# A depthwise convolution issued to VectorE one instruction at a time, paced by the matmuls traced, instead of as one late block

## The chip, the core and the metric

The kernel runs on one core of a Trainium2 chip. A core has a matrix engine (TensorE, PE in the profile), a vector engine (VectorE, DVE), a scalar engine (ScalarE, ACT), GpSimd (POOL) and SyncE (SP), which here mostly issues DMAs. Each engine works through its own list of instructions in the order of the program; engines wait for each other by semaphores. The metric is the device time of one execution in microseconds (us), taken as the median of several runs.

## The reference

One decoder layer, for 1024 prompt tokens and 64 sample tokens (8 requests of 8), 1088 columns in all, in fp32:

```python
xn = rmsnorm(x, norm1_g)
q, k, v, glu_a, glu_b, gate_a, gate_b = jnp.split(xn @ w_in, SPLIT_IDX, axis=-1)
branch_a = attend(q, k, v, window=128, sinks) @ w_o_attn      # 16 query heads, 4 kv heads
u = glu_a * jax.nn.sigmoid(glu_b)                             # the gated branch, 1024 channels
c = dwconv_valid(concat([past, u]), conv_b_w, conv_b_bias)    # 31 taps, each channel by itself
branch_b = jax.nn.silu(layernorm(c, ln_b_g, ln_b_b)) @ w_pb
h = x + (sigmoid(gate_a) * branch_a + sigmoid(gate_b) * branch_b) @ w_out
y = rmsnorm(h + conv_ffn(rmsnorm(h, norm2_g)), norm_f_g)
```

The change concerns `c`, the convolution over 31 taps of the 1024 channels of `u`.

## The kernel before

Channels lie on the 128 partitions, tokens along the free dimension. Every fp32 product is three matmuls of rounded operands: high word of the weight with high word of the input, high with low, low with high (L200, L201, L202, in `mm3`). A weight block is split into its two words when it is near its turn: ACT writes the high word `whi` (L181), DVE the low word `wlo` (L182), one *unit* ahead of the unit that multiplies by it.

The input projection is a list of units, in the order of a table: 8 blocks of `glu_b` and `glu_a` (b, a), q, k, v, and 16 gates (g). A unit is one block of 128 output columns: `stream` runs over three pieces of 384, 384 and 320 tokens and, in each, over 8 blocks of the contraction. A piece has one of four PSUM buffers called `mm`, which is read out by ACT or DVE and then used again four pieces later. Four more, called `aux`, serve the attention. The two v units stand in a loop of their own, `do_v`: 9 products of 128 tokens by 256 columns, each split into two words by ACT and DVE (`split_ps`, L229 and L230). The gate units and q units of this stage are called by their letters below; "the q stage" is the run of q and k units of the second half of the heads, from about 347 us to 440 us.

The attention steps (scores, softmax, transposes of the probabilities `p`, their split into `pth` and `ptl` at L229 and L230, and the product with v that gives `av`, L385) hang on an agenda: `tick`, called by `stream` once for every three matmuls, issues those that are due between the matmuls of the units.

When a block of `glu_a` is done, `a_done` calls `conv(i, u)` for its 128 channels. It writes, all on DVE: two products and two sums for the sample tokens (L486, L487), one sum of odd and even columns (L488), 44 multiply-adds over 512 columns (L480, tiles `bt`, `c`), four closing instructions (L499 to L502); ACT writes three start values, and POOL's queue stores the result for the LayerNorm, which loads it at about 633 us. So 53 DVE instructions a block, 424 over the 8 blocks.

The text of the program is not the order of the engines' lists: a scheduler at build time places each instruction by a number, its priority, which grows as the program is traced, and by its own estimate of when engines are free. `later(off)` adds an offset to that number:

```python
with self.later(CONV_LATER):      # CONV_LATER = 1200
    self.conv(i, u)
```

So before the change the whole convolution of a block is traced at once and stands 1200 numbers later: the scheduler puts its instructions where it believes DVE is free.

Of the kernel before, what the change touches and what calls it, by code (L numbers as in the profile page):

```python
# [70 lines left out]
MEAN_LATER = (100, 100, 100)  # L71
W_PARTS = 4
PIECES = {384: 3, 320: 4, 432: 4, 256: 2, 272: 4}
CONV_LATER = 1200
LN_STEPS = (0, 7, 15)
LN_LEAD = -4
LN_SPACING = 15
# [4 lines left out]
def weight_order():  # L82
    order, count = [], {}
    gates = [(kind, i) for i in range(KT) for kind in ("ga", "gb")]
    for w in SEQUENCE:
        n = count[w] = count.get(w, -1) + 1
        if w == "g":
            order.append(gates.pop(0))
        elif w[0] == "q":
            order.append(("q", (int(w[1]), n)))  # L90
        elif w[0] == "k":
            order.append(("k", int(w[1])))
        else:
            order.append((w, n))
    assert not gates
    n_in = len(order)
    order += [("o", m) for m in range(KT)]
    order += [("pb", m) for m in PB_ORDER]
    order += [("out", m) for m in range(KT)]
    for f in range(NF):  # L100
        order += [("up", f), ("up", NF + f)]
    order += [("dn", f) for f in range(NF)]
    return order, n_in
# [16 lines left out]
class Build:  # L120
    def __init__(self, tc, a):
        self.tc, self.nc, self.a = tc, tc.nc, a
        self.order, self.n_in = weight_order()
        self.uid = 0
        self.agenda, self.now = [], 0

    @contextmanager
    def later(self, off):
# [329 lines left out]
    def tick(self, upto=None):  # L458
        self.now = self.now + 1 if upto is None else upto
        while self.agenda and self.agenda[0][0] <= self.now:  # L460
            self.agenda.pop(0)[1]()

    def drain(self):
        while self.agenda:
            self.agenda.pop(0)[1]()


    def conv(self, i, u):
        nc = self.nc
        half = SEQ // 2  # L470
        acc = self.t(self.cv, [P, T], "c")
        sm = self.t(self.cv, [P, half + 15], "sm")
        bt = self.t(self.cv, [P, half + 1], "bt")
        us = u[:, PW:].rearrange("p (b t) -> p b t", b=NB)
        sp = acc[:, SEQ:].rearrange("p (b t) -> p b t", b=NB)
        ev, od = u[:, 0:PW:2], u[:, 1:PW:2]
        ye, yo = acc[:, 0:SEQ:2], acc[:, 1:SEQ:2]
        h = lambda k: self.c("cw", i * CW + k)
        hs = lambda j: self.hsum[:, 16 * i + j:16 * i + j + 1]
        mac = lambda o, x, w: nc.vector.scalar_tensor_tensor(o, x, w, o, ALU.mult, ALU.add)  # L480
        taps = self.c("cw", i * CW, CW)[:, None, None, :].to_broadcast([P, NB // 2, NT, CW])
        prod = acc[:, 0:NS // 2 * CW].rearrange("p (b t k) -> p b t k", b=NB // 2, k=CW)
        for x in range(2):
            win = us[:, 4 * x:4 * x + 4, 0:NT]
            win = bass.AP(tensor=win.tensor, offset=win.offset, ap=[list(z) for z in win.ap] + [[1, CW]])
            nc.vector.tensor_tensor(prod, win, taps, ALU.mult)  # L486
            nc.vector.tensor_reduce(sp[:, 4 * x:4 * x + 4, :], prod, AX.X, ALU.add)  # L487
        nc.vector.tensor_tensor(sm, od[:, 0:half + 15], ev[:, 1:half + 16], ALU.add)  # L488
        act = nc.scalar.activation
        act(bt, ev[:, 0:half + 1], AF.Identity, scale=h(0))  # L490
        act(ye, od[:, 0:half], AF.Identity, bias=self.c("cb", i), scale=h(1))
        act(yo, sm[:, 0:half], AF.Identity, bias=self.cb2[:, i:i + 1], scale=hs(0))
        for j in range(1, 16):
            mac(bt, ev[:, j:j + half + 1], h(2 * j))
            if j < 15:
                mac(ye, od[:, j:j + half], h(2 * j + 1))
            mac(yo, sm[:, j:j + half], hs(j))
        out = u[:, NS:NS + SEQ]
        nc.vector.tensor_scalar(u[:, 0:NS], acc[:, SEQ:], self.c("cb", i), None, ALU.add)  # L499
        nc.vector.tensor_tensor(yo, yo, bt[:, 1:], ALU.subtract)  # L500
        nc.vector.tensor_tensor(out[:, 1::2], yo, ye, ALU.subtract)
        nc.vector.tensor_tensor(out[:, 0::2], ye, bt[:, 0:half], ALU.add)  # L502
        nc.gpsimd.dma_start(self.d_c[i, :, 0:SEQ], out)
        nc.gpsimd.dma_start(self.d_c[i, :, SEQ:], u[:, 0:NS])
# [116 lines left out]
    def folds(self, n_dn):  # L621
        wall = self.a["wall"]

        def stages(n):
            x, y = wall[n_dn + 2 * n], wall[n_dn + 2 * n + 1]
            return self.fold_stages(x[:, :HW], y[:, :HW], x[:, HW:], y[:, HW:], self.d_wd[n])

        ticks = [[] for _ in range(NF - PLAIN)]
        for n in range(NP):
            for k, stage in enumerate(stages(n)):  # L630
                ticks[n * (NF - PLAIN - 6) // (NP - 1) + k] += stage
        for tick in ticks:
            self.fold(tick)
            yield

    def pool(self, es, name, side="right", bufs=1):
        return es.enter_context(self.tc.tile_pool(name=name, bufs=bufs, side=side, reuse_waits="tile"))

    def phase_x(self):
# [14 lines left out]
        def u_views(u):  # L654
            return u[:, PW:].rearrange("p (b t) -> p b t", b=NB)

        def u_start(i):
            u = self.t(self.cv, [P, UW], "u", bufs=2)
            nc.gpsimd.memset(u[:, 0:HIST], 0.0)
            nc.gpsimd.memset(u[:, HIST + SEQ:PW], 0.0)  # L660
            nc.sync.dma_start(u_views(u)[:, :, 0:HIST], a["cbT"][i])
            return u
# [23 lines left out]
        def a_done(i, u):  # L686
            us = u_views(u)
            nc.gpsimd.dma_start(a["o_cbp"][i], u[:, SEQ:SEQ + HIST])
            nc.gpsimd.dma_start(a["o_cbs"][i], us[:, :, NT:])
            with self.later(CONV_LATER):  # L690
                self.conv(i, u)

        def do_b(i):
            u = u_start(i)
            self.stream(("b", i), xs, b_evac(u))
            gate_u(u)
            return u

        def do_a(i, u):
            self.stream(("a", i), xs, a_evac(u))  # L700
            a_done(i, u)
# [108 lines left out]
        while len(self.w_raw) < FIRST:  # L810
            self.w_load()
        xr.append(self.norm1_load(p0, 2))
        u = u_start(0)
        a_t = self.t(self.cv, [P, T], "c")
        self.scale = None
# [34 lines left out]
        for d, x, y, r in u_part(u, 0, T):  # L850
            nc.vector.tensor_tensor(d, d, r(a_t[:, x:y]), ALU.mult)
        a_done(0, u)
        self.scale = None
        p0_es.close()
# [9 lines left out]
        for n, (kind, i) in enumerate(self.order[:self.n_in]):  # L864
# [16 lines left out]
            if kind == "b":  # L881
                u = do_b(i)
# [19 lines left out]
    def phase_y(self, right, a0_es, states, ah, al):  # L902
        nc, tc, a, pool = self.nc, self.tc, self.a, self.pool
        s_es = ExitStack()
        sp = pool(s_es, "s", "left")
        sh, sl = self.act_tiles(sp, "s")
        bh, bl = states[1]["q"]

        def xa(c, k):
            o, n = CHUNKS[c]  # L910
            h, l = (ah, al) if k < 4 else (bh, bl)
            return h[:, k % 4, o:o + n], l[:, k % 4, o:o + n]

        def do_o(m):
            t = self.t(self.lt, [P, T], "ga", bufs=2)
            nc.sync.dma_start(t, self.d_ga[m])
            nc.scalar.activation(t, t, AF.Sigmoid)

            def ev(c, o, n, ps):
                r = self.t(self.lt, [P, 384], "ma", bufs=2)  # L920
                nc.vector.tensor_tensor(r[:, :n], ps[:, :n], t[:, o:o + n], ALU.mult)
                nc.gpsimd.dma_start(self.d_ma[m, :, o:o + n], r[:, :n])

            self.stream(("o", m), xa, ev)

        steps = []
        for x in range(KT):
            steps += self.ln_steps(x, self.now + LN_LEAD + x * LN_SPACING, sh, sl)
        self.plan(steps)
        for m in range(KT):  # L930
            do_o(m)
        self.drain()
        a0_es.close()
        right.close()
        self.phase_z(s_es, sh, sl)
# [855 lines left out]
```

## Time and profile before

| | |
|---|---|
| time, median of 3 runs (lowest, highest) | 1659.28 us (1658.15, 1660.51) |
| the profiled execution | 1659.53 us, span 1657.8 us, granted clock 0.997 |
| PE busy | 1642.9 us, 99% of the span |
| DVE busy | 1336.1 us, 81% |
| ACT busy | 893.3 us, 54% |
| POOL busy | 328.1 us, 20% |
| input projection with attention and convolution | about 45 to 616 us |

The times of the trace start with the span, which is 1.7 us shorter than the execution that it belongs to. A row of the timeline gives an instruction's start, its length, its engine, its line, and in brackets the idle time ahead of it and what ended that. A matmul's length covers more than its turn: the turns are read from the starts (384 columns: 0.173 us apart). The same holds on DVE, where a multiply-add is 0.75 us long, and the next starts 0.67 us after it.

### The profile page before, as it was taken

What the parts mean: (1) busy time and instruction counts of PE and PEld (TensorE: products, weight loads), DVE (VectorE), ACT (ScalarE), POOL (GpSimd) and SP (SyncE); (2) the same over time, 40 slices, a digit from 0 to 9 for tenths busy, and PEclk for the clock granted to TensorE, in tenths of its full rate; (3) what the DMA queues carried; (4) which work ended last, traced back from release to release, by engine and by line L of the source; (5) the groups of instructions that cost most, each with busy time, mean ns of one, the idle gap of its engine ahead of it and who ended that gap; (6) DMA issues with size and microseconds to landing.
All of it is one profiled execution on the core that took longest, in us unless ns stands there. A gap on an engine that the chain in (4) does not pass through costs nothing.

```text
span 1657.8 us, 30344 instructions
## 1 busy us (share of the span) xinstructions
PE 1642.9 (99%) x11616; PEld 1627.3 (98%) x11616; DVE 1336.1 (81%) x2430; ACT 893.3 (54%) x1817; POOL 328.1 (20%) x589
## 2 busy tenths in 40 slices
PE   9999999999999999999999999999999999999998
PEld 9999999999999999999999999999999999999997
DVE  8899999999769995866685897877777777977556
ACT  7434477753488754993343564444444446834322
POOL 1210114171211211110000123333433220000050
PEclk9999999999999999999999999999999999999999
DMA  6122216254421255545346527676777544857473
GB/s 213 43 52 71 60 63 167 62 178 103 115 67 47 83 195 184 165 137 190 113 136 194 134 79 204 183 182 176 182 176 176 144 112 149 286 157 218 138 148 117
DMA packets 121313, 232.12 MB, mean 140 GB/s; under 512 B 25408, under 2 KB 67536, under 8 KB 120736
## 3 DMA queue, kind: packets, MB, share of 16 engines
q1 hardware_dynamic: 88208, 140.14, 27.6%
q0 software_dynamic: 32384, 89.51, 21.3%
q8 instruction: 91, 1.49, 0.4%
q10 hardware_dynamic: 576, 0.53, 0.1%
q14 instruction: 54, 0.44, 0.1%
HBM read 169.74 MB, written 89.62 MB: 156 GB/s over the span
## 4 chain that ended last, share of the span: by engine, by line
PE 81%; DVE 11%; ACT 4%; issue 2%; DMA 1%; POOL 0%; SPq 0%; DVEq 0%; ACTq 0%; POOLq 0%
PE mm L200 19%; PE mm L202 19%; PE mm L201 19%; PE aux L200 6%; PE aux L202 6%; PE aux L201 6%; DVE c L480 3%; DVE bt L480 2%; PE aux L366 1%; ACT p L332 1%; ACT p L336 1%; PE aux L378 1%; DVE wlo L182 1%; PE aux L356 1%; PE aux L379 1%
## 5 line engine op out<-in xcount | busy, mean ns | idle before, releaser
L200 PE MATMUL mm<-xh,whi 128*128 128x384 f32 (+1 forms) x920 | 306.6, 333 | 0.6 <-ACT whi L181 0.6
L201 PE MATMUL mm<-xl,whi 128*128 128x384 f32 (+1 forms) x920 | 301.1, 327 | 0.0
L202 PE MATMUL mm<-xh,wlo 128*128 128x384 f32 (+1 forms) x920 | 300.7, 327 | 0.0
L200 PEld LDWEIGHTS mm<-xh,whi 128*128 128x128 f32 x920 | 173.3, 188 | 2.2 <-ACT whi L181 1.2
L201 PEld LDWEIGHTS mm<-xl,whi 128*128 128x128 f32 x920 | 173.4, 188 | 1.0
L202 PEld LDWEIGHTS mm<-xh,wlo 128*128 128x128 f32 x920 | 173.1, 188 | 0.1
L1209 DVE SCALAR_TENSOR_TENSOR acc<-st,fc,acc 128x1104 f32<-128x1104 f32 x88 | 119.5, 1361 | 8.7 <-ACT acc L1207 7.9
L181 ACT CAST whi<-wraw 128x1024 fp32r<-128x1024 f32 (+1 forms) x65 | 62.7, 970 | 56.8 <-PE mm L201 44.6
L480 DVE SCALAR_TENSOR_TENSOR bt<-u,consts,bt 128x513 f32<-128x513 f32 x120 | 89.7, 747 | 0.6
L480 DVE SCALAR_TENSOR_TENSOR c<-sm,hsum,c 128x512 f32<-128x512 f32 x120 | 89.4, 745 | 0.5
L182 DVE TENSOR_TENSOR wlo<-wraw,whi 128x1024 fp32r<-128x1024 f32 (+1 forms) x65 | 72.5, 1121 | 20.1 <-ACT whi L181 19.6
L480 DVE SCALAR_TENSOR_TENSOR c<-u,consts,c 128x512 f32<-128x512 f32 x112 | 83.5, 745 | 0.2
L229 ACT CAST wlo<-th 128x512 fp32r<-128x512 f32 x56 | 35.1, 626 | 65.0 <-PE aux L202 41.3
L1378 ACT COPY st<-mm 128x272 f32<-128x272 f32 (+2 forms) x133 | 44.4, 350 | 46.8 <-PE mm L202 46.8
L200 PE MATMUL mm<-th,whi 128*128 128x272 f32 x240 | 69.3, 289 | 0.0
L202 PE MATMUL mm<-th,whi 128*128 128x272 f32 x240 | 69.3, 289 | 0.0
L201 PE MATMUL mm<-tl,whi 128*128 128x272 f32 x240 | 69.1, 288 | 0.0
L332 ACT ACTIVATE p<-p,nm 128x257 f32<-128x257 f32 (+1 forms) x128 | 62.2, 490 | 11.0 <-DVE nm L327 10.1
L1357 DVE TENSOR_TENSOR st<-st,aux 128x272 f32<-128x272 f32 (+2 forms) x95 | 34.2, 378 | 38.5 <-PE aux L202 38.5
L202 PE MATMUL mm<-sh,wlo 128*128 128x384 f32 (+1 forms) x192 | 62.6, 326 | 0.0
L201 PE MATMUL mm<-sl,whi 128*128 128x384 f32 (+1 forms) x192 | 62.6, 326 | 0.0
L200 PE MATMUL mm<-sh,whi 128*128 128x384 f32 (+1 forms) x192 | 62.6, 326 | 0.0
(651 smaller groups left out, 5906.8 us busy)
## 6 DMA issues: line engine op xcount, KB each, us to landing
wraw<-wall SPq DMA_DIRECT2D x87, 512.0 KB, 4.0
d_x<-st POOLq DMA_DIRECT2D x27, 544.0 KB, 4.9
d_wd<-wall POOLq DMA_DIRECT2D x54, 256.0 KB, 6.1
th<-wall SPq DMA_DIRECT2D x18, 512.0 KB, 6.0
wraw<-wall SPq DMA_DIRECT2D x33, 256.0 KB, 4.1
x<-d_x SPq DMA_DIRECT2D x14, 544.0 KB, 4.8
d_x<-acc POOLq DMA_DIRECT2D x9, 816.0 KB, 7.2
d_wo<-wall POOLq DMA_DIRECT2D x24, 256.0 KB, 4.9
```

Of the source, the lines that this page charges most:

```text
L181: self.nc.scalar.copy(h[:, z], r[:, z])
L182: self.nc.vector.tensor_tensor(l[:, z], r[:, z], h[:, z].bitcast(F32), ALU.subtract)
L200: mm(ps, wh, xh, start=first, stop=False, skip_group_check=more)
L201: mm(ps, wh, xl, start=False, stop=False, skip_group_check=more)
L202: mm(ps, wl, xh, start=False, stop=last, skip_group_check=more)
L229: self.nc.scalar.copy(h, src)
L332: nc.scalar.activation(pt[:, j, lo:width + 1], pt[:, j, lo:width + 1], AF.Exp, bias=nm[:, j:j + 1], scale=-1.0, accum_out=den[:, j:j + 1])
L336: nc.scalar.activation(pt[:, j, lo:width], pt[:, j, lo:width], AF.Identity, scale=den[:, j:j + 1])
L480: mac = lambda o, x, w: nc.vector.scalar_tensor_tensor(o, x, w, o, ALU.mult, ALU.add)
L1209: self.last_tap = nc.vector.scalar_tensor_tensor(acc, st[:, k:k + AW], fw(f, k), acc, ALU.mult, ALU.add)
L1357: plus = lambda d, s: nc.vector.tensor_tensor(d, d, s, ALU.add)
L1378: op(d, r(ps))
```

## The change

`conv` becomes a generator, which stops after each of its DVE instructions (some stops hold two). `a_done` only puts it on a list. `tick`, after the attention steps that are due, calls a new function `pace`. This looks at the instructions traced since the last call: each of PE adds 0.172 to an account, each of DVE takes 0.5 off; the account is capped at 1.4, and while it is above zero, one step of the oldest convolution is issued and 0.68 taken off. Each step is tied (`issue_after`) behind the DVE instruction traced last, with an offset of 30 instead of 1200. Starting a new block of `glu_b` first issues what is left of all convolutions but the last, and the phase after the projection issues everything that is left.

```diff
-CONV_LATER = 1200
+PE_STEP, DVE_STEP, CONV_STEP = 0.172, 0.5, 0.68
+ROOM = 1.4
+PACE_LATER = 30
...
     def tick(self, upto=None):
...
             self.agenda.pop(0)[1]()
+        self.pace()
+
+    def pace(self):
+
+        traced, pe, dve = self.nc.cur_bb.bb.instructions, self.nc.tensor.engine, self.nc.vector.engine
+        for ins in list(traced)[self.seen:]:
+            if ins.engine == pe:
+                self.room += PE_STEP
+            elif ins.engine == dve:
+                self.room -= DVE_STEP
+        self.seen = len(traced)
+        self.room = min(self.room, ROOM) if self.convs else 0
+        while self.convs and self.room > 0:
+            self.conv_step()
+            self.room -= CONV_STEP
+        self.seen = len(traced)
+
+    def conv_step(self):
+        with ExitStack() as es:
+            dve = self.nc.vector.engine
+            es.enter_context(self.tc.issue_after(next(x for x in reversed(list(self.nc.cur_bb.bb.instructions)) if x.engine == dve)))
+            es.enter_context(self.later(PACE_LATER))
+            if next(self.convs[0], None) is None:
+                self.convs.pop(0)
+
+    def conv_flush(self, keep=0):
+        while len(self.convs) > keep:
+            self.conv_step()
...
         for j in range(1, 16):
+            yield 1
             mac(bt, ev[:, j:j + half + 1], h(2 * j))
+            yield 1
             if j < 15:
                 mac(ye, od[:, j:j + half], h(2 * j + 1))
+                yield 1
             mac(yo, sm[:, j:j + half], hs(j))
...
         def u_start(i):
+            self.conv_flush(1)
...
-            with self.later(CONV_LATER):
-                self.conv(i, u)
+            self.convs.append(self.conv(i, u))
```

Every engine gets the same instructions as before; only their order differs. The first place is DVE's list around the v products, which before stand between multiply-adds of the convolution (L480; `wlo` is the low word of a weight, L327 a row of scores). `do_v` does not call `tick`. Before:

```order
L230 TENSOR_TENSOR v_944<-mm_1856,v_944 128x2x128
L480 SCALAR_TENSOR_TENSOR bt_1131<-u_947,consts_77,bt_1131 128x513
L480 SCALAR_TENSOR_TENSOR c_1129<-u_947,consts_77,c_1129 128x512
L480 SCALAR_TENSOR_TENSOR c_1129<-sm_1130,hsum_86,c_1129 128x512
L480 SCALAR_TENSOR_TENSOR bt_1131<-u_947,consts_77,bt_1131 128x513
L230 TENSOR_TENSOR v_944<-mm_1883,v_944 128x2x128
L480 SCALAR_TENSOR_TENSOR c_1129<-sm_1130,hsum_86,c_1129 128x512
L499 TENSOR_SCALAR u_947<-c_1129,consts_77 128x64
L500 TENSOR_TENSOR c_1129<-c_1129,bt_1131 128x512
L502 TENSOR_TENSOR u_947<-c_1129,bt_1131 128x512
L230 TENSOR_TENSOR v_944<-mm_1910,v_944 128x2x128
```

The same place now (the lines are numbered anew: L480 is L512, L230 is L233, L182 is L185, L327 is L330):

```order
L512 SCALAR_TENSOR_TENSOR c_1457<-u_886,consts_77,c_1457 128x512
L233 TENSOR_TENSOR v_883<-mm_1663,v_883 128x2x128
L233 TENSOR_TENSOR v_883<-mm_1690,v_883 128x2x128
L233 TENSOR_TENSOR v_883<-mm_1717,v_883 128x2x128
L233 TENSOR_TENSOR v_883<-mm_1744,v_883 128x2x128
L233 TENSOR_TENSOR v_883<-mm_1771,v_883 128x2x128
L233 TENSOR_TENSOR v_883<-mm_1798,v_883 128x2x128
L233 TENSOR_TENSOR v_883<-mm_1825,v_883 128x2x128
L233 TENSOR_TENSOR v_883<-mm_1852,v_883 128x2x128
L185 TENSOR_TENSOR wlo_185_1917<-wraw_1657,whi_184_1916 128x1024
```

All eight v splits stand in a row, with no step of the convolution between them. What was between them stands later in DVE's list.

The second place is DVE's list in the q stage, around the 25th low word of the projection, before (L728 splits a piece of q):

```order
L480 SCALAR_TENSOR_TENSOR bt_4194<-u_4012,consts_77,bt_4194 128x513
L480 SCALAR_TENSOR_TENSOR c_4192<-u_4012,consts_77,c_4192 128x512
L728 TENSOR_TENSOR q_518_4254<-mm_4418,q_518_4254 64x256
L182 TENSOR_TENSOR wlo_535_4453<-wraw_4354,whi_534_4452 128x1024
L728 TENSOR_TENSOR q_519_4255<-mm_4418,q_519_4255 64x256
L480 SCALAR_TENSOR_TENSOR c_4192<-sm_4193,hsum_86,c_4192 128x512
```

and now (L728 is L768):

```order
L512 SCALAR_TENSOR_TENSOR c_4210<-u_3979,consts_77,c_4210 128x512
L768 TENSOR_TENSOR q_515_4193<-mm_4385,q_515_4193 64x256
L185 TENSOR_TENSOR wlo_535_4425<-wraw_4313,whi_534_4424 128x1024
L768 TENSOR_TENSOR q_516_4194<-mm_4385,q_516_4194 64x256
L512 SCALAR_TENSOR_TENSOR c_4210<-sm_4211,hsum_86,c_4210 128x512
```

Here the two lists look alike again. How many of the 424 instructions of the convolution stand ahead of a given instruction in DVE's list:

| instruction | starts before the change at | ahead, before | ahead, now |
|---|---|---|---|
| the last v split | 187.49 us | 108 | 84 |
| 15th low word | 278.89 us | 174 | 146 |
| 19th low word | 345.49 us | 218 | 202 |
| 20th low word | 359.86 us | 234 | 229 |
| 25th low word | 422.54 us | 299 | 300 |
| 34th low word | 561.54 us | 361 | 370 |

So the multiply-adds taken out of the v products are all put in again by the 25th low word, most of them between the 15th and the 20th.

More of the change, by code (lines that the diff above doesn't have):

```diff
@@ L125, in __init__ @@
         self.agenda, self.now = [], 0
+        self.convs, self.seen, self.room = [], 0, 0
     @contextmanager
@@ L493, in conv @@
         for j in range(1, 16):
+            yield 1
             mac(bt, ev[:, j:j + half + 1], h(2 * j))
+            yield 1
             if j < 15:
                 mac(ye, od[:, j:j + half], h(2 * j + 1))
+                yield 1
             mac(yo, sm[:, j:j + half], hs(j))
+        yield 1
         out = u[:, NS:NS + SEQ]
@@ L500, in conv @@
         nc.vector.tensor_tensor(yo, yo, bt[:, 1:], ALU.subtract)
+        yield 1
         nc.vector.tensor_tensor(out[:, 1::2], yo, ye, ALU.subtract)
+        yield 1
         nc.vector.tensor_tensor(out[:, 0::2], ye, bt[:, 0:half], ALU.add)
@@ L924, in do_o @@
             self.stream(("o", m), xa, ev)
+        self.conv_flush()
         steps = []
```

## The prediction

> **What bounds the kernel now.** I read the page's engine table and the chain first, then busy time by stage, then the places where PE waits.
>
> ```profile
> PE 1642.9 (99%) x11616; PEld 1627.3 (98%) x11616; DVE 1336.1 (81%) x2430; ACT 893.3 (54%) x1817; POOL 328.1 (20%) x589
> ...
> PE 81%; DVE 11%; ACT 4%; issue 2%; DMA 1%; POOL 0%; SPq 0%; DVEq 0%; ACTq 0%; POOLq 0%
> PE mm L200 19%; PE mm L202 19%; PE mm L201 19%; PE aux L200 6%; PE aux L202 6%; PE aux L201 6%; DVE c L480 3%; DVE bt L480 2%; PE aux L366 1%; ACT p L332 1%; ACT p L336 1%; PE aux L378 1%; DVE wlo L182 1%; PE aux L356 1%; PE aux L379 1%
> ```
>
> PE is idle for 1657.8 − 1642.9 = 14.9 us of the span, so no order of instructions can gain much; it can lose more. DVE is on the chain with 11%, and the multiply-adds of the convolution (L480) are its largest rows there. Where, the stretches of the input projection tell (PE, PEld, DVE, ACT, POOL busy, clock, DMA share, GB/s):
>
> ```profile
> core 0: us, PE busy (x) PEld busy (x) DVE busy (x) ACT busy (x) POOL busy (x), PEclk, DMA share, GB/s
> ...
> 150.00:190.00 40.00, 40.00 (x310) 40.00 (x310) 39.97 (x65) 8.95 (x19) 3.92 (x8) 1.00 0.23 61
> 190.00:250.00 60.00, 57.61 (x360) 55.58 (x359) 59.24 (x141) 46.22 (x123) 11.08 (x18) 0.97 0.20 62
> 250.00:300.00 50.00, 49.94 (x325) 48.36 (x325) 47.83 (x107) 41.21 (x105) 17.78 (x33) 1.00 0.55 139
> 300.00:347.00 47.00, 47.00 (x306) 45.39 (x305) 44.87 (x103) 34.55 (x87) 13.38 (x27) 1.00 0.40 107
> 347.00:385.00 38.00, 38.00 (x235) 37.96 (x234) 37.84 (x59) 12.36 (x21) 26.59 (x30) 1.00 0.53 160
> 385.00:442.00 57.00, 57.00 (x349) 57.00 (x348) 53.47 (x79) 19.02 (x38) 8.99 (x16) 1.00 0.42 101
> 442.00:485.00 43.00, 42.83 (x276) 41.87 (x274) 19.67 (x60) 34.69 (x93) 6.36 (x13) 1.00 0.38 95
> 485.00:545.00 60.00, 59.90 (x392) 57.93 (x391) 58.06 (x135) 51.04 (x129) 9.85 (x18) 1.00 0.17 47
> 545.00:605.00 60.00, 59.92 (x387) 58.04 (x386) 57.91 (x129) 46.16 (x119) 10.74 (x21) 1.00 0.31 99
> ```
>
> From 150 to 442 us both engines are nearly full: in 292 us PE lacks 2.4 us and DVE 0.03 + 0.76 + 2.17 + 2.13 + 0.16 + 3.53 = 8.8 us. Only in 442 to 485 has DVE air (19.67 of 43). PE runs through because DVE is late for nothing that PE needs at once: products wait in PSUM buffers, and low words are made a unit ahead. All but 0.1 us of it lies in one stretch, at one wait:
>
> ```profile
> PE aux L356 <- DVE ptl L230: 2.3, 2, 2.2
> ...
> 201.04 0.33 PE L202 MATMUL mm<-xh,wlo 128*128 128x384 f32 x1
> 203.52 0.38 PE L356 MATMUL aux<-kd,q 128*128 128x256 f32 x1 [2.15 <-DVE ptl L230]
> ...
> 205.27 0.52 PE L200 MATMUL mm<-xh,whi 128*128 128x384 f32 x1
> 205.59 0.52 PE L201 MATMUL mm<-xl,whi 128*128 128x384 f32 x1
> ...
> 207.51 0.51 PE L201 MATMUL mm<-xl,whi 128*128 128x384 f32 x1
> 207.83 0.36 PE L202 MATMUL mm<-xh,wlo 128*128 128x384 f32 x1
> ```
>
> The scores need an `aux` buffer that DVE empties with `ptl` (L230), and this stands behind a row of multiply-adds, because DVE is late:
>
> ```profile
> 199.47 0.75 DVE L480 SCALAR_TENSOR_TENSOR c<-u,consts,c 128x512 f32<-128x512 f32 x1
> 200.14 0.75 DVE L480 SCALAR_TENSOR_TENSOR c<-sm,hsum,c 128x512 f32<-128x512 f32 x1
> ...
> 202.79 0.68 DVE L230 TENSOR_TENSOR ptl<-aux,pth 128x512 fp32r<-128x512 f32 x1
> ```
>
> The starts are 0.67 us apart: this is what a step of the convolution costs DVE below.
>
> **The change part by part.** Nothing is added or removed on any engine; POOL's stores, SP's loads and ACT's start values of the convolution move with it. So the sum has the terms of moved DVE work only.
>
> *The v products: DVE catches up.* Before, they lie between the multiply-adds and are split late:
>
> ```profile
> 182.47 0.41 DVE L230 TENSOR_TENSOR v<-mm,v 128x256 fp32r<-128x256 f32 x1
> ...
> 187.49 0.41 DVE L230 TENSOR_TENSOR v<-mm,v 128x256 fp32r<-128x256 f32 x1
> 187.82 1.16 DVE L487 TENSOR_REDUCE c<-c 128x32 f32<-128x992 f32 x1
> ...
> 181.74 0.28 PE L200 MATMUL mm<-whi,xh 128*128 128x256 f32 x1
> 179.11 0.37 ACT L229 CAST v<-mm 128x256 fp32r<-128x256 f32 x1 [2.46 <-PE mm L202]
> ```
>
> PE begins the ninth product at 181.74, so the eighth is done then; ACT's copy takes 0.37 us, and the last split can stand at about 182.3 instead of 187.49: a lead of 5.2 us. For that, 24 steps fewer lie ahead of it (108 before, 84 now), 24 × 0.67 = 16 us of work put off. DVE has 8 splits of 0.4 us in that stage and idles for the rest; this idle time does not come back.
>
> *The wait at 201 us goes.* The `ptl` has to come 2.15 us sooner, and the lead is 5.2 us, with no more steps between the last v split and it than before (13 now, 15 before). If it goes, its slow matmuls go with it: 2.4 us of idle PE (60 − 57.61) and a clock of 0.97 over 60 us, 1.8 us more. Bounds: 0 if 3 us of the lead are lost again, −4.2 us if all goes. I take −4.2.
>
> The Trainium skill ("TensorE: Matmul & The Clock Gate", Part 1, the HAM clock gate) has the clock fall after an idle window of about 3.4 us. By it a wait of 2.15 us would leave the clock alone, and the term would be −2.4; the trace here shows matmuls 0.32 us apart instead of 0.17 after just that wait, so the row decides.
>
> *The work put off comes due.* Its price is read where the low words are needed, at the units' starts:
>
> ```profile
> 345.49 1.23 DVE L182 TENSOR_TENSOR wlo<-wraw,whi 128x1024 fp32r<-128x1024 f32 x1 [0.21 <-ACT whi L181]
> ...
> 359.86 1.23 DVE L182 TENSOR_TENSOR wlo<-wraw,whi 128x1024 fp32r<-128x1024 f32 x1
> ...
> 422.54 1.23 DVE L182 TENSOR_TENSOR wlo<-wraw,whi 128x1024 fp32r<-128x1024 f32 x1
> 423.79 0.43 DVE L728 TENSOR_TENSOR q<-mm,q 64x256 fp32r<-64x256 f32 x1
> ...
> 417.36 0.34 PE L200 MATMUL mm<-xh,whi 128*128 128x384 f32 x1
> 429.22 0.34 PE L200 MATMUL mm<-xh,whi 128*128 128x384 f32 x1
> 429.57 0.35 PE L202 MATMUL mm<-xh,wlo 128*128 128x384 f32 x1
> ```
>
> These are the 19th, 20th and 25th low word. The 25th is finished at 423.77 and first used by the third matmul of the unit at 429.57: a slack of 5.8 us. The piece of q that is split at 423.79 was finished on PE when the unit of 417.36 began, and its buffer is wanted again four pieces on, at 429.22: 5.0 us. So DVE may be some 5 to 6 us late there before PE stops.
>
> How late is it? From the last v split to the 25th low word there are 299 − 108 = 191 steps before and 300 − 84 = 216 now: 25 × 0.67 = 16.8 us more. The lead takes off 5.2, leaving 11.6. What of DVE's idle time can be filled: 7.5 us lie between 190 and 422 (0.76 + 2.17 + 2.13 + 0.16, and 37.5 of 57 parts of 3.53). But to the 19th low word there are 218 − 108 = 110 steps before and 118 now, 8 × 0.67 = 5.4 us, just the lead: up to 345 us DVE is ahead of or level with what it was, and idle time there is waiting for data, which no early start fills:
>
> ```profile
> L327 DVE CUSTOM_DVE_ANT_0 p<-aux,masks,nsink 128x256 f32<-128x256 f32 x34 | 14.6, 478 | 0.4 <-PE aux L357 0.2
> L385 DVE TENSOR_TENSOR av<-aux,av 64x512 f32<-64x512 f32 x11 | 7.6, 687 | 1.8 <-ACT av L384 1.6
> L728 DVE TENSOR_TENSOR q<-mm,q 64x384 fp32r<-64x384 f32 (+1 forms) x22 | 11.4, 519 | 1.7 <-ACT q L727 1.1
> ```
>
> (the first two of 250 to 347 us, the third of 385 to 442). From the 19th on DVE is behind, and 0.16 + 2.3 = 2.5 us can be filled. So it is 11.6 − 2.5 = 9.1 us late at the 25th low word, and 11.6 if nothing is filled; with all 7.5 filled, 4.1. Less the slack of 5.0 (the PSUM buffer, the tighter one): PE starts that unit later than before by −0.9 us to +6.6 us, by my reading +4.1. The gain of 4.2 us at 201 is already in this: PE then runs into DVE's lateness and its own lead is used up.
>
> I take +4, between these, since both the idle time that can be filled and the lateness come from rows of this stretch. After 442 DVE has 23 us of air and is level again.
>
> *The second attention stretch, 485 to 605.* Here the change puts steps earlier, not later: 9 more ahead of the 34th low word (6 us of DVE work), in a stretch where DVE is idle for 1.94 + 2.09 = 4.0 of 120 us, and PE loses 0.2. Between 0 (low words a unit ahead, buffers four pieces) and 6 us less those 4.0 of air and the slack; I take +0.5, near the end of no loss, as the slack of about 5 us in the other stretch is more than the 2 us left.
>
> *What moves beside it, at nothing.* The last convolution ends no later than before (the counts meet), so POOL's stores are there for the LayerNorm at 633 us. ACT's three start values per block stand between copies; ACT is busy 54%, and if one held a copy up, it would add to DVE's lateness by its 0.8 us at most.
>
> The sum against the profiled execution (1659.53, its span and 1.7 us around it): −4.2 + (4.2 + 4.1) + 0.5 = +4.6, so 1664.1; the median of the runs is 0.25 us lower. I say 1664.
>
> **The rivals.**
>
> *DVE's lateness is absorbed.* If DVE fills the 7.5 us of idle time or the scheduler's new order of PE asks for the attention's rows later, the low end of −0.9 holds: about 1658.5, no change. For it: slack of 5 to 6 us per unit. Against it: 5.06 us of that idle time lie where DVE is not late.
>
> *Faster.* The wait at 201 goes and DVE's lateness at every unit stays under 5 us less 4.2: then all of it is kept, 1659.5 − 4.2 = 1655.3. This decides at 0.8 us of lateness against the old times at the 25th low word, where I count 9.1. For it speaks that the lists may let steps of the convolution run while PE waits for nothing; a miscount of 8 us of DVE time in 235 us, 3%, would do.
>
> *More stalls.* Nothing filled (+6.6 in the q stage), each stop of PE followed by slow matmuls as at 205 us (1.8 us a time), and the second stretch short by 2 to 4 us: 1659.5 + 6.6 + 1.8 + 3 = 1671. For it: a 2.15 us wait was enough for the slow clock. Against: while DVE sets the pace, a slower PE only fills the wait.
>
> **How the numbers follow.** Likeliest, DVE late in the q stage: 0.50, 1664 with its own range of 1661 to 1668. Absorbed: 0.25, 1657 to 1662. Faster: 0.14, 1655.3. More stalls: 0.11, 1671. A measurement here can tell 0.2% (3.3 us) from no change, so the same is 1656.0 to 1662.6: the absorbed case. Faster 0.14, same 0.25, slower 0.61. The range reaches from 1656.5, which leaves out the faster case, to 1670.5, which leaves out the half of the stalls: 1656.5 to 1670.5.
>
> **What the profile after would show.** DVE idle by some 10 us or more in 165 to 187, with eight v splits in a row; no wait of PE for `ptl` at 201, and a clock of 1.00 in 190 to 250; DVE at 97% or more from 350 to 435; waits of PE for low words (`wlo`) or for a buffer that a split of q empties, 6 to 9 us in all, in 360 to 435; little in 485 to 605. I am wrong if DVE in the q stage still idles by 2 us and PE waits for nothing there (then it is faster), or if PE's waits lie elsewhere, at the attention's `aux` buffers.

## The result and the profile after

The changed kernel takes 1684.12 us (median of 4 runs, 1682.27 to 1685.46), the kernel before on the same chip 1659.89 us: a ratio of 1.0146, 95% interval 1.0129 to 1.0164. It is 24 us slower. The forecast was 1664, 5 us slower, with 1670.5 as the upper end: the direction held, the size did not.

The profiled execution's span is 1680.3 us against 1657.8. Its engine table, then the same stretches as in the prediction (45 to 107 us is new, and 605 to 660):

```profile
PE 1650.1 (98%) x11616; PEld 1629.9 (97%) x11616; DVE 1336.5 (80%) x2430; ACT 895.0 (53%) x1817; POOL 323.2 (19%) x589
...
45.00:107.00 62.00, 60.53 (x386) 60.10 (x385) 52.06 (x85) 28.30 (x56) 18.22 (x19) 1.00 0.22 52
107.00:150.00 43.00, 43.00 (x264) 43.00 (x264) 41.92 (x62) 18.68 (x40) 2.32 (x6) 1.00 0.17 56
150.00:190.00 40.00, 37.44 (x290) 37.05 (x289) 28.42 (x51) 11.06 (x22) 5.01 (x9) 1.00 0.26 63
190.00:250.00 60.00, 59.88 (x385) 58.23 (x384) 57.06 (x126) 45.54 (x118) 13.89 (x25) 1.00 0.37 96
250.00:300.00 50.00, 49.87 (x320) 47.66 (x319) 46.61 (x106) 36.28 (x87) 16.27 (x29) 1.00 0.46 125
300.00:347.00 47.00, 45.71 (x295) 44.06 (x294) 45.86 (x105) 31.75 (x86) 11.08 (x18) 1.00 0.35 83
347.00:385.00 38.00, 32.54 (x185) 30.70 (x185) 34.65 (x61) 19.86 (x44) 17.70 (x33) 0.91 0.51 158
385.00:442.00 57.00, 53.46 (x310) 52.32 (x309) 55.96 (x84) 15.11 (x29) 5.98 (x11) 0.97 0.31 74
442.00:485.00 43.00, 43.00 (x276) 42.99 (x275) 29.49 (x66) 25.74 (x71) 6.92 (x14) 1.00 0.39 107
```

DVE does the same work in all (1336.5 us busy, 1336.1 before), but later: 28.42 of 40 us in the v stage where it was 39.97, and from 442 to 485 us it is busy for 29.49 us where it was 19.67. PE stands where it ran through before: in 347 to 442 us it lacks 9.0 us and runs at a clock of 0.91 and 0.97. The wait at 201 us is gone (59.88 of 60 us, clock 1.00). The largest waits of PE, over the whole span:

```profile
PE mm L205 <- DVE wlo L185: 4.5, 3, 3.0
PE aux L561 <- DVE red L554: 4.0, 1, 4.0
PE mm L203 <- ACT qs L773: 2.8, 2, 2.6
PE mm L203 <- DVE v L233: 2.3, 1, 2.3
PE aux L432 <- ACT sp L339: 1.6, 1, 1.6
```

The list of the `mm` matmuls is the same in both kernels, so the same matmul can be looked up in both traces. Its start moves by +0.3 us at 167 us (times of before), +3.4 at 182, +0.2 at 205, +16.2 at 429, +16.1 at 619, +21.0 at 653 and +22.4 at 655, and stays there to the end (+22.6). So there are three losses, in the v stage (3.1), in the q stage (17, after the gain of 4.2 at 201 us had made good the first loss) and at the LayerNorm (6), and little between. A first part of the 17 comes just ahead of the q stage: at 306.39 us PE waits 1.3 us for the 16th low word, which is 5.9 us late (45.71 of 47 us busy in 300 to 347).

*The v stage.* The first v split before, then DVE's timeline with the row of v splits now, and PE's, which shows who waits for the first of them:

```profile
168.21 0.41 DVE L230 TENSOR_TENSOR v<-mm,v 128x256 fp32r<-128x256 f32 x1
```

```profile
172.51 0.75 DVE L512 SCALAR_TENSOR_TENSOR c<-u,consts,c 128x512 f32<-128x512 f32 x1
173.17 1.42 DVE L233 TENSOR_TENSOR v<-mm,v 128x256 fp32r<-128x256 f32 x4
177.20 0.42 DVE L233 TENSOR_TENSOR v<-mm,v 128x256 fp32r<-128x256 f32 x1 [2.61 <-ACT v L232]
...
185.70 0.42 DVE L233 TENSOR_TENSOR v<-mm,v 128x256 fp32r<-128x256 f32 x1 [2.41 <-ACT v L232]
187.80 1.23 DVE L185 TENSOR_TENSOR wlo<-wraw,whi 128x1024 fp32r<-128x1024 f32 x1 [1.68 <-ACT whi L184]
...
173.65 0.39 PE L203 MATMUL mm<-whi,xh 128*128 128x256 f32 x1 [2.27 <-DVE v L233]
```

The first four splits come at once at 173.17, behind all the multiply-adds; the first stood at 168.21 before. By then four products fill the four `mm` buffers, and PE waits 2.27 us to write the fifth.

*The q stage.* The 20th and the 25th low word, and the matmuls that wait for the one and use the other:

```profile
377.54 1.22 DVE L185 TENSOR_TENSOR wlo<-wraw,whi 128x1024 fp32r<-128x1024 f32 x1
...
444.19 1.23 DVE L185 TENSOR_TENSOR wlo<-wraw,whi 128x1024 fp32r<-128x1024 f32 x1
...
378.81 0.69 PE L205 MATMUL mm<-xh,wlo 128*128 128x384 f32 x1 [3.05 <-DVE wlo L185]
445.80 0.35 PE L205 MATMUL mm<-xh,wlo 128*128 128x384 f32 x1
```

They are 17.7 and 21.7 us later than before (359.86 and 422.54).

*The LayerNorm.* SP's loads and what PE waits for, first of the kernel before, then of the changed one:

```profile
600.73 0.40 SPq L879 DMA_DIRECT2D ah<-d_ah  x1
632.98 0.37 SPq L526 DMA_DIRECT2D ct<-d_c  x1
```

```profile
634.98 0.38 SPq L919 DMA_DIRECT2D ah<-d_ah  x1
656.41 0.37 SPq L566 DMA_DIRECT2D ct<-d_c  x1
...
673.84 0.47 PE L561 MATMUL aux<-red,mean 128*128 128x136 f32 x2 [4.04 <-DVE red L554]
674.75 0.53 PE L204 MATMUL mm<-q,whi 128*128 128x384 f32 x1
```

The load of attention's output (`ah`, six pieces with `al`) starts 34 us later, twice PE's lateness, and the load of the convolution's result 23 us later. The matmuls after the wait stand 0.32 us apart.

### The profile page after: what moved, and what is told of

The parts are those of the page before. It is cut to its first block, busy times and chain, and to the rows that moved or that the text cites. A ratio compares the mean times of both kernels' runs of the same rounds, so it can differ in the third digit from the quotient of the medians.

```text
span 1680.3 us, 30306 instructions
## 1 busy us (share of the span) xinstructions
PE 1650.1 (98%) x11616; PEld 1629.9 (97%) x11616; DVE 1336.5 (80%) x2430; ACT 895.0 (53%) x1817; POOL 323.2 (19%) x589
## 4 chain that ended last, share of the span: by engine, by line
PE 78%; DVE 11%; issue 3%; ACT 3%; DMA 2%; POOL 0%; SPq 0%; DVEq 0%; POOLq 0%; ACTq 0%
PE mm L203 18%; PE mm L205 18%; PE mm L204 18%; PE aux L203 6%; PE aux L205 6%; PE aux L204 6%; DVE c L512 4%; DVE bt L512 2%; PE aux L369 1%; DVE q L768 1%; DVE wlo L185 1%; PE aux L359 1%; PE aux L360 1%; PE aux L381 1%; DMA xr<-xT 1%
## 5 line engine op out<-in xcount | busy, mean ns | idle before, releaser
L205 PE MATMUL mm<-xh,wlo 128*128 128x384 f32 (+1 forms) x920 | 304.1, 331 | 4.5 <-DVE wlo L185 4.5
L512 DVE SCALAR_TENSOR_TENSOR bt<-u,consts,bt 128x513 f32<-128x513 f32 x120 | 89.8, 749 | 0.4
L512 DVE SCALAR_TENSOR_TENSOR c<-sm,hsum,c 128x512 f32<-128x512 f32 x120 | 89.6, 746 | 0.3
L185 DVE TENSOR_TENSOR wlo<-wraw,whi 128x1024 fp32r<-128x1024 f32 (+1 forms) x65 | 72.6, 1122 | 15.0 <-ACT whi L184 13.7
L512 DVE SCALAR_TENSOR_TENSOR c<-u,consts,c 128x512 f32<-128x512 f32 x112 | 83.5, 746 | 1.2 <-ACT c L525 0.9
```

Of the source, the lines that this page charges most:

```text
L185: self.nc.vector.tensor_tensor(l[:, z], r[:, z], h[:, z].bitcast(F32), ALU.subtract)
L205: mm(ps, wl, xh, start=False, stop=last, skip_group_check=more)
```

## The experiments

Three things differ between the kernels: when a step is traced, the tie behind DVE's last instruction, and the offset (30 or 1200). The time of the kernel before in the runs' company was 1659.4 to 1660.4 us.

**One difference at a time.** e1 fills the hole in the v stage, e2 restores the offset, e3 drops the tie, e4 does the first two.

```diff
# e1, in do_v's loop (pace takes the credit per matmul as an argument)
+                    self.pace(0.119)
# e2
-PACE_LATER = 30
+PACE_LATER = 1200
# e3, in conv_step
-            es.enter_context(self.tc.issue_after(next(x for x in reversed(...) if x.engine == dve)))
# e4: the edits of e1 and e2
```

> The changed kernel, with pace also called in the v products' loop (0.119 us credited per matmul there), so that steps of the convolution stand between the v splits again: 106 of 424 ahead of the last v split, against 84 in the changed kernel and 108 before. Theory A (the steps kept out of the v products come due in the q stage): the 17 us that PE loses there go to 5 or less; the first v split stays late (the wait of 2.3 us in the v stage stays), the LayerNorm's wait of 4 us stays since attention ends as late in PE's list: 1668 us, 1663 to 1672. Rival C (attention placed later in the lists, by the convolution's priority next to its own, is what costs, hole or no hole): 1676 or more.

Measured: 1677.59 us, ratio 1.0106 (1.0091 to 1.0121). Filling the hole takes only 6.5 of the 24 us away. That is outside theory A's range and inside rival C's: a miss. With the small offset, the hole is the smaller part of the price. DVE is busy for 39.97 us in the v stage again, but lags elsewhere (55.09 of 60 us in 190 to 250, 45.39 of 50 in 250 to 300); the wait for the first v split (2.3 us), one for low words (6.3 us in all) and the LayerNorm's (4.5 us) are there.

> The changed kernel with one number changed: the priority offset of a step is 1200 as before instead of 30; the tie stays. The hole in the v stage stays (84 steps ahead of the last v split), attention stands in PE's and DVE's lists where it stood before, and the steps put off are made up only in the air after 442 us (271 ahead of the 25th low word, 299 before, 300 in the changed kernel). Theory A with attention's delay as its other half: no stall in the q stage, no wait at 201 us, LayerNorm as before: 1655 us, 1652 to 1660. Rival H (the hole alone is what costs): DVE does 16 us less in the v stage as in the changed kernel, and the time stays at 1672 or more.

Measured: 1662.74 us, ratio 1.0014 (1.0005 to 1.0024). Same hole, and nearly all of the loss is gone: rival H falls, though theory A's range ended at 1660. The gain of 4 us at 201 does not last either: PE is 2.1 us ahead of the kernel before at 303 us, and behind it from about 466 us on, where it waits 2.0 us for softmax's `p` of the second half.

> The changed kernel without the tie behind the last DVE instruction; steps traced by pace and priority offset 30 stay. DVE's list up to 442 us is then that of before (108 steps ahead of the last v split, 300 ahead of the 25th low word); in the second attention stretch up to 16 steps stand earlier and attention ends 33 matmuls later in PE's list (56 in the changed kernel). Theory A (tie makes hole and delay): 1660 to 1665, the wait at 201 us back. Rival C (the pace's trace order and the small offset do it): 1675 or more.

Measured: 1661.92 us, ratio 1.0014 (1.0004 to 1.0024). Tracing in small steps with the small offset costs 2 us by itself; up to 442 us the scheduler puts the steps where it put them before, and the wait at 201 us is back (2.2 us). Rival C as it stands here falls: it takes the tie and the small offset together. In the first half attention is not late in this run, so whether its lateness alone would cost as much is left to e5 and e9.

> Both edits: pace called in the v loop, and offset 1200. 100 steps ahead of the last v split, 287 ahead of the 25th low word (299 before), attention where it stood before. Theory A: DVE does a little less than before everywhere up to the q stage's end and loses little, no wait at 201 us if the last v split comes earlier than before: 1655 to 1659. Rival H: as before, 1659. Rival C is not at stake. LayerNorm's wait is absent as before.

Measured: 1662.3 us, ratio 1.0017 (1.0008 to 1.0027): no better than before, and above theory A's range; at 203.54 us PE waits 1.5 us for `ptl`, the old wait in a new place.

**The parts alone, on the kernel before.** e5 delays attention, e6 and e7 make the hole.

```diff
# e5, in tick, while the first half's attention runs
-            self.agenda.pop(0)[1]()
+            with self.later(60 if self.late else 0):
+                self.agenda.pop(0)[1]()
# e6, e7: conv as a generator; of the second block 31 (e6) or 44 (e7) steps are traced in a_done,
# the rest and the third block after do_v, tied behind the last v split, at the old priority
```

> The kernel before, with one edit: the attention steps of the first half of the heads get a priority offset of 60, so that in PE's list they come some 55 matmuls (about 9.5 us) later; the convolution stands as before (108 of 424 steps ahead of the last v split, 294 ahead of the 25th low word). No hole, no tie. At the 19th low word 400 other DVE instructions stand ahead instead of 419 (408 in the changed kernel). Theory D (attention's delay brings its DVE work into the q stage, where DVE has no room, and PE waits for low words and buffers): 1666 us, 1662 to 1674, with the waits between 350 and 440 us. Rival P (delay alone is harmless, only together with the steps of the convolution forced early): 1658 to 1661.

Measured: 1661.5 us, ratio 1.0015 (1.0006 to 1.0024). Theory D falls, a miss: attention late by itself is nearly harmless. Its products with v stand 40 to 64 of the `mm` matmuls later all through the first half; in the changed kernel that grows from nothing to some 80 at its end, so the delays are alike in size, not in course.

> The kernel before, with the hole alone: the steps of the second and third convolution that stood between the v splits are tied behind the last v split, at their old priorities. 84 steps ahead of the last v split (108 before), 276 ahead of the 25th low word (299 before), attention where it was. Theory D: the wait at 201 us goes, the backlog runs on at low priority into the air after 442 us, no stall in the q stage: 1655 us, 1653 to 1660. Rival H (DVE time lost in the v stage costs by itself, as the prediction's sum had it): 1662 or more.

Measured: 1664.58 us, ratio 1.0028 (1.0016 to 1.0039), not the 1655 expected: a second miss. The wait at 201 us goes and the q stage has no stall, as theory D had it, but the loss comes where I saw air, from 442 to 485 us:

```profile
442.00:485.00 43.00, 38.67 (x224) 35.98 (x223) 28.11 (x70) 31.47 (x86) 6.84 (x15) 0.96 0.37 92
...
PE aux L368 <- ACT p L338: 3.0, 2, 1.9
PE aux L358 <- ACT kd L772: 1.1, 1, 1.1
```

There the second half's attention starts, and DVE is busy with the backlog (28.11 us instead of 19.67); its first splits and softmax come late.

> As the run before, with 13 steps left between the v splits: 97 steps ahead of the last v split instead of 84, 289 ahead of the 25th low word. DVE then is about even with the v products at the last split and loses less. Theory D: the wait at 201 us goes, 1655 us, 1653 to 1659, a version that beats the kernel before. Rival: the wait comes back somewhere near, at an aux buffer, and the time is 1658 to 1661.

Measured: 1660.82 us, ratio 1.0005 (0.9996 to 1.0014), no change. PE is 5.3 us ahead of the kernel before until 454 us, and then loses it all, so theory D misses a third time and its rival holds (in 442 to 485 us PE is busy for 40.25 of 43 us, at a clock of 0.96). In DVE's timeline the first q split after 440 us stands at 440.07, against 440.20 before: DVE is not ahead at all, and the second half's attention can't start sooner than DVE lets it. So removing the wait at 201 us brings nothing by itself here. No version of this study beats the kernel before.

**What fills the q stage.** e9 and e10 leave 24 steps (12 taps of two blocks) out of the convolution, in the changed kernel and in the kernel before, so that its result is incomplete.

```diff
-            if j < 15:
+            if j < 15 and not (i in (2, 3) and j <= 12):
                 mac(ye, od[:, j:j + half], h(2 * j + 1))
```

> The changed kernel with 24 of the 424 steps left out (12 taps of the third and of the fourth convolution, so the convolution is incomplete), all of them due between the last v split and the 25th low word: 276 ahead of that low word instead of 300, 16 us less work for VectorE; attention's places in the lists as in the changed kernel. Theory S (from 170 to 440 us the list of VectorE is full, and every idle microsecond on it is paid for at the low words of the q stage): the 16 us that PE is behind at 440 us go to 0 to 4, the LayerNorm's loss stays: 1667 us, 1664 to 1671. Rival C (attention's later places make the stalls, whatever VectorE has to do): 1678 or more.

Measured: 1670.89 us, ratio 1.0062 (1.0044 to 1.008). The same matmul at 430 us is now 3.3 us late instead of 16.2, and PE has no wait in the q stage:

```profile
347.00:385.00 38.00, 38.00 (x239) 37.22 (x239) 37.03 (x68) 19.34 (x47) 15.65 (x30) 1.00 0.40 131
385.00:442.00 57.00, 57.00 (x345) 56.73 (x344) 55.80 (x84) 18.48 (x36) 11.08 (x19) 1.00 0.46 109
...
PE aux L561 <- DVE red L554: 5.1, 1, 5.1
PE mm L203 <- DVE v L233: 2.3, 1, 2.3
```

16 us less work for DVE gives PE 13 us back, as theory S has it; v stage and LayerNorm keep their losses. In PE's list attention's products stand as late as in the changed kernel (up to 85 matmuls), so rival C falls in its other form too: lateness in the list alone is not the price.

> The kernel before with the same 24 steps left out. Theory S: nothing waits in the q stage before, so only the wait at 201 us could go, and it lies ahead of the steps left out: 1659 us, 1656 to 1661, as before within 0.2%. If VectorE's fullness cost the kernel before something that no wait of PE shows, 1655 or less.

Measured: 1660.3 us, ratio 1.0001 (0.9992 to 1.0011). The same 16 us are worth nothing in the kernel before. The 13 us are thus not the price of the work but of its having come too late.

> The changed kernel with an offset of 100 instead of 30 and the tie kept. Attention comes up to 31 matmuls later than before in the first half (60 in the changed kernel, 0 with 1200), 292 steps stand ahead of the 25th low word (300 in the changed kernel, 271 with 1200). Theory S: between the two, nearer to the run with 1200, since steps may run into the time after 442 us: 1667 us, 1663 to 1673. Rival (it is the tie, at any offset that keeps the convolution near): 1678 or more.

Measured: 1669.3 us, ratio 1.0057 (1.0041 to 1.0073). A dose between e2 and the changed kernel gives a time between: attention's products up to 39 matmuls late in the first half instead of some 80, PE 3.7 us late at 430 us and 9.1 at 619.

**The LayerNorm.** e8 moves its steps, e11 the convolution's end, e13 and e14 set the offset by block.

```diff
# e8
-LN_LEAD = -4
+LN_LEAD = 24
# e11
+            if n == self.n_in - LAST_GATES - 2:
+                self.conv_flush()
# e13 (e14: > 5 instead of < 6); a list entry is (block, generator)
-            es.enter_context(self.later(PACE_LATER))
+            es.enter_context(self.later(PACE_LATER if self.convs[0][0] < 6 else 1200))
```

> The changed kernel, with the LayerNorm's steps 28 ticks (84 matmuls, 14.6 us) later among the matmuls of the o-projection. Theory L (the conv's results come late through a full DMA, and the LayerNorm's sums make PE wait 4.0 us and run with a slow clock for 1.4 after): that wait goes, 1678.5 us, 1677 to 1680. Rival: the steps that follow them come late instead at the o-projection's end, no gain: 1683 to 1686.

Measured: 1687.0 us, ratio 1.0164 (1.0147 to 1.0181). The rival: PE gains 5 us at the LayerNorm's sums, where it waits 1.4 us instead of 4.0, and loses 7 to 8 around 777 us, where it waits 4.3 us for the LayerNorm's result (`sh`).

> The changed kernel with all open steps of the convolution issued two units ahead of the place where attention is drained, so that 20 more of them stand ahead of the 37th low word and the last convolution is finished some 10 us sooner; attention's end is put 16 matmuls (2.8 us) further back by it. Theory L (the LayerNorm's sums come late because the last convolution's result reaches the memory late, among the loads of attention's output): the wait of 4.0 us at 674 us and the slow clock behind it go: 1678 us, 1676 to 1681. Rival: attention's end, still later, is what the o-projection then waits for: 1684 or more.

Measured: 1694.47 us, ratio 1.0206 (1.0189 to 1.0222). The LayerNorm's wait is gone, but with DVE's list full of the flushed steps, attention stops PE for 11.4 us (`aux` L381 waiting for `av`). The number is the rival's. The run doesn't tell theory L from others, as PE is another 17 us later there (the matmul of 619 us is 33.3 us late).

> The changed kernel with offset 30 for the first six convolutions only and 1200 for the last two: up to 485 us its lists are those of the changed kernel; in the second attention stretch attention ends where it did before (matmul 2922 of PE's mm list, 2978 in the changed kernel), and the last convolution's steps stand a little later than in the changed kernel (398 of 424 ahead of the 37th low word, 404 in the changed kernel). Theory M (attention's late end brings its loads of 4.4 MB into the way of the convolution's store and loads): the wait of 4.0 us at the LayerNorm and its slow clock go: 1678 us, 1676 to 1680. Rival (the last convolution's lateness makes it): 1683 to 1687.

Measured: 1678.71 us, ratio 1.0113 (1.0096 to 1.0129), 5.4 us less than the changed kernel. PE's largest waits no longer hold the LayerNorm's. POOL issues the last store of the convolution and SP the load after it:

```profile
649.07 0.54 POOL L543 DMA_DIRECT2D d_c<-u  x1 [1.39 <-DVE u L542]
...
618.91 1.25 SPq L919 DMA_DIRECT2D ah<-d_ah  x1
651.95 0.37 SPq L566 DMA_DIRECT2D ct<-d_c  x1
```

In the changed kernel this store is issued at the same time:

```profile
649.71 0.54 POOL L543 DMA_DIRECT2D d_c<-u  x1 [0.59 <-DVE u L542]
```

So by the clock the convolution ends as late as there, and still the load can go 4.5 us sooner (651.95 against 656.41): the store takes 2.9 us to land instead of 6.7, in e13 and in the changed kernel:

```profile
d_c<-u POOLq DMA_DIRECT2D x1, 512.0 KB, 2.9
```

```profile
d_c<-u POOLq DMA_DIRECT2D x1, 512.0 KB, 6.7
```

What differs is the load of attention's output, at 618.91 instead of 634.98. In 640 to 660 us the DMA engines are busy for 0.96 in the changed kernel and for 0.69 in e13. Theory M holds for the larger part, the 3.8 us of the landing. The convolution's lateness has a smaller one: the matmul of 640 us (times of before) is 18.1 us late in e13 and 16.9 in the changed kernel, so measured against PE the store is issued 1.8 us sooner in e13. No run separates the two.

> The reverse: offset 1200 for the first six convolutions and 30 for the last two. Up to 485 us the lists are those of the run with 1200 throughout (1662.7 us), after that those of the changed kernel. Theory M: the LayerNorm's loss of 5 to 6 us alone on top of that: 1668 us, 1666 to 1670. Rival (the loss there was a result of the 16 us lost earlier): 1662 to 1664.

Measured: 1670.18 us, ratio 1.0065 (1.005 to 1.008): the wait at L561 is there with 4.9 us, and the time is 7.4 us above e2's with nothing lost in the q stage. The two halves account for the whole to within 2.5 us: 19.3 us lost in e13 and 7.4 more in e14 than in e2 make 26.7, where the changed kernel loses 24.2.

## Why the prediction was wrong

*The wait at 201 us goes: right*, and with it the slow clock, 4.2 us.

*The v products, wrong by its lead.* I looked at the last split alone, with 24 steps fewer ahead of it. The first has 2 more (84 against 82), and DVE came there later, as it had 2.6 us less to do from 45 to 107 us (52.06 against 54.70). I had not looked at that stretch, nor at the buffers that the first split frees. The lead at the last split is 1.8 us (185.70 against 187.49) instead of 5.2, and PE loses 3.1 us where I had no term. The two are one: each later split follows PE's product (before the last one DVE idles for 2.41 us), and PE is 3.4 us late there.

*The work put off comes due: right in its mechanism, with the slack right and the lateness mis-sized.* The 25th low word is 21.7 us late where I had 9.1; PE is 16.2 late there, a difference of 5.5, the slack that I read. Two terms failed:

- the lead, by 3.4 us, as above;
- the idle time. I let DVE fill 2.5 us more than before; instead it idles more. Summed over DVE's rows of the timeline, it idles for 12.5 us between the last v split and the 20th low word, 5.2 before, so 7.3 more: it waits for ACT's high words, for softmax, for scores, for ACT's part in splitting attention's output. Each step is tied behind the DVE instruction traced last, so steps that could fill a gap may stand behind the one that waits; without the tie (e3) DVE idles for 5.1 us there, as before. Nor is DVE level up to 345 us, as I had it: the 16th low word is 5.9 us late (305.12 against 299.24), the 19th 2.3. With 2.5 and 7.3 the term is off by 9.8, with the lead by 13.2, about the 12.6 missing.

The sum behind it: I counted only the convolution's steps ahead of the low words. At the 15th low word there stand 296 other DVE instructions ahead, 318 before; at the 19th 406 and 417; at the 20th 423 in both. So 17 other instructions, attention's above all (6 before), and 27 steps (16 before) lie between the 19th and the 20th low word, and these are 29.8 us apart (347.75 and 377.54) instead of 14.4. In PE's list attention's products with v are up to some 80 matmuls later. In e2 and e3 those of the first half are no later than before, and in e12 half as much: it is the tie with the small offset that does this. e5 shows that a delay of attention alone costs some 2 us, and in e9, with attention as late in the list and 16 us less of steps, PE is 3.3 us late at 430 us. So the full price comes when both halves, steps and attention, must be done by the same low words.

*The second attention stretch: right*; the matmul at 619 us is as late as the one at 485.

*What moves beside it, at nothing: wrong.* I followed the convolution's end and POOL's stores, and not attention's end, which the loads of `ah` and `al` wait for. Attention's last matmul moves back 76 matmuls in the list, and 6 us are lost at the LayerNorm (e13, e14). The convolution's end was not level either: its last store is issued at 649.71 us instead of 630.10, 19.6 us later, where PE is 16.9 us late.

Of the rivals, "more stalls" was nearest, at 1671 with 0.11; its price of the second stretch was put in the wrong place. "Faster" fails as its own condition said: DVE was late by 22 us, not 0.8.

What stays open: why PE gains nothing in e2 and e4, where no low word is late. The waits for softmax's `p` (e2) and for `ptl` (e4) that take the place of the old one were seen, and not taken away; e7 points to DVE's list, which is no further ahead at 440 us when PE is. Open too is how the 6 us at the LayerNorm divide between the store's landing and the convolution's end.

## What to carry to other kernels

Where two engines are both full, count for the one that feeds the other *all* its instructions ahead of each deadline, not only those that a change moves: a tie that raises one kind of work pushes another kind back, and idle time at one place is paid for at the next deadline. A gap in a full engine's list costs little as long as the work may run on at low priority past the deadline (3 us of 16 in e2, 5 in e6), and nearly its whole length when it has to be made up ahead of it (13 of 16 between the changed kernel and e9). Follow the end of every chain that moves to the transfers that wait for it; a load that starts 17 us later than the matmuls around it can land in the way of another.

## What the runs showed of the hardware

The same wait of 2.27 us in the v stage was followed by a full clock in the changed kernel and e11, and by a slow one in e1, e8, e9 and e13; these are 170 to 180 us of the changed kernel and of e13:

```profile
170.00:180.00 10.00, 7.73 (x65) 7.52 (x64) 5.01 (x10) 1.11 (x3) 1.36 (x3) 1.00 0.56 118
```

```profile
170.00:180.00 10.00, 7.73 (x53) 7.52 (x52) 5.30 (x10) 0.74 (x2) 1.63 (x3) 0.83 0.60 120
```

The Trainium skill ("TensorE: Matmul & The Clock Gate", Part 1) says that the window in which activity is measured runs freely and does not start with the kernel, so that the place of the first matmul in it shifts the change of clock. If the same goes for a pause, it fits these rows, where one wait has two outcomes. The same part of the Trainium skill has the clock fall after an idle window of some 3.4 us; that does not fit: here 2.27 us were enough in four runs of six. The slow clock cost 1.5 us more (4.1 us lost at the wait instead of 2.6).
